# One rotation for queries and keys, moved ahead of the compressions, in a hybrid attention and recurrence kernel

## The chip, the cores and the metric

One core of one Trainium2 chip runs the whole program. The metric is the device time of one execution in microseconds (us), lower is better.

## The reference, cut to what matters

One layer on 1024 tokens of width 1024, float32. A combined projection of the normalised input feeds two groups of eight heads of 64.

```
q, kc, vc, ks, vs, kw, vw, gates, g_nsa, rwkv_in, g_rwkv = split(rms_norm(x) @ w_in)
# group A: three attention branches, 8 query heads, 2 key heads each
k_cmp, v_cmp = compress(kc), compress(vc)        # blocks of 32, stride 16, two-layer MLP
o_cmp = softmax(q @ k_cmp) @ v_cmp               # unrotated q; its weights also pick 8 blocks of 64 keys
o_sel = softmax(rope(q) @ rope(ks) over the picked blocks) @ vs
o_win = softmax(rope(q) @ rope(kw) over the last 512 keys) @ vw
# group B: RWKV-7, a state of 64x64 per head, one step per token (here in chunks of 64)
state = state*w - (state@kk) (kk*a) + v k ;  y = state @ r
out = rms_norm(x + concat(o_nsa*silu(g_nsa), o_rwkv*silu(g_rwkv)) @ w_out)
```

`rope` turns the first 16 of a head's 64 rows: row d becomes `a*cos + w*sin`, where `a` is the row and `w` the row eight further on or back (the sign is in the sine table). The kernel keeps queries and keys in two float32r parts, a high part (`dQH`, `dKH`) and the remainder (`dQL`, `dKL`).

## The kernel before, in words

**Order of the work.** First the normalised input is transposed and a projection of 29 groups of columns begins; each group is 48 matmuls of 512 columns (`p_q`, `p_gn`, `p_gr` and so on), and its weights are fetched in two halves, split in two parts by ScalarE (ACT) and VectorE (DVE). These matmuls are the *filler*: `filler.step(n)` puts n of them at a place in the order of TensorE (PE), `filler.through(name)` all up to a group. The recurrence runs in eight *units* of 128 tokens by half the heads; each unit is a chain of twelve steps (`weave`), each step a few small matmuls (`pc`, `py`) whose results go through DVE and ACT copies (`z`, `x`) before the next step, and after them a half share of the filler, side work, and the other half. Units are counted from 0 in the code (`n`); "the sixth unit" here is n = 6, "the seventh" n = 7, the last.

**Side work.** In unit n < 7 GpSimd (POOL) computes the 31-step triangular recursion of the next unit, two small operations per step on tiles `la`, `lt` and `ltmp` (lines 587 and 589), eight groups of steps with the last three steps at step 5. Its result goes to DRAM (`dT<-lt`) and back (`tt<-dT`), is transposed on DVE (line 633) and enters the matmuls `px` (step 10) and `pt12` (step 11). In units 6 and 7 the two compressions are woven in: each loads two key tiles (`kc2`) and four weight tiles (`w1`), and runs four quarters of 16 matmuls (`pcm`), each behind a pair of additions on DVE and POOL (`xc`). After them, in unit 7, come the rotations: of the keys of both branches (64 rows used), and, started at step 7, of the queries (128 rows). All of these tiles come from one pool of six 4 KB tiles (`c4`), taken in turn.

**What follows.** After unit 7 and its norm a *prologue* loads the queries of the first tile of 128 tokens (`load_queries`: `qt` unrotated, `q1`, `q2`), the keys (`load_keys`) and values, and runs for this tile the compressed branch (`compressed`: matmuls `pcs`, `pct`, `poc`) and the row maxima of both other branches (`row_max`: `pd`, `ps`, reduced on DVE to `bm`), mixed with the filler that is left. Then the attention loop runs over eight tiles in the order `TILES = (1, 5, 4, 3, 6, 2, 7, 0)`; beside each tile it does the compressed branch and the row maxima of the next one, and later the output projection with `w_out`.

**Who sets the order.** In the units the order of PE and POOL is the order in which the program is written; in the prologue and the attention that of PE alone. The other engines, and SP, whose queue issues every DMA, are ordered by a planner that simulates the program; each engine then works strictly in its order. A tile that is placed where an older tile lay waits for the last use of that one.

## Time and profile before

| | |
|---|---|
| median of three runs | 1079.12 us (1078.54 to 1079.7) |
| the profiled execution | 1082.96 us |
| its span, first to last instruction | 1081.2 us |
| PE busy | 936.9 us, 87% of the span |
| DVE, ACT, POOL busy | 579.8, 333.1, 451.6 us |
| mean granted clock of TensorE | 0.934 of full speed |

All rows below are of the profiled execution. "Idle before" is the time in which an engine did nothing ahead of an instruction, with what ended it.

### The profile page before, as it was taken

What the parts mean: (1) busy time and instruction counts of PE and PEld (TensorE: products, weight loads), DVE (VectorE), ACT (ScalarE), POOL (GpSimd) and SP (SyncE); (2) the same over time, 40 slices, a digit from 0 to 9 for tenths busy, and PEclk for the clock granted to TensorE, in tenths of its full rate; (3) what the DMA queues carried; (4) which work ended last, traced back from release to release, by engine and by line L of the source; (5) the groups of instructions that cost most, each with busy time, mean ns of one, the idle gap of its engine ahead of it and who ended that gap; (6) DMA issues with size and microseconds to landing.
All of it is one profiled execution on the core that took longest, in us unless ns stands there. A gap on an engine that the chain in (4) does not pass through costs nothing.

```text
span 1081.2 us, 17166 instructions
## 1 busy us (share of the span) xinstructions
PE 936.9 (87%) x6353; PEld 665.6 (62%) x6353; DVE 579.8 (54%) x1241; ACT 333.1 (31%) x648; POOL 451.6 (42%) x738
## 2 busy tenths in 40 slices
PE   5999999679999899899997619758999999889976
PEld 4888877556766676577775417435555555555555
DVE  7532355344746466464443305447667884776444
ACT  5432323122342434233121101334333344223321
POOL 3100118374555538454513320266545456236521
PEclk9899999689999899899998869879999999899989
DMA  7433344413444355525753395551103132321021
GB/s 248 115 103 111 105 134 135 104 47 102 120 104 122 103 152 139 140 79 138 191 152 112 114 208 114 167 144 59 40 20 98 35 84 50 88 49 56 32 88 39
DMA packets 154381, 114.61 MB, mean 106 GB/s; under 512 B 54961, under 2 KB 132858, under 8 KB 154298
## 3 DMA queue, kind: packets, MB, share of 16 engines
q1 hardware_dynamic: 154298, 113.52, 38.8%
q8 instruction: 50, 0.82, 0.3%
q14 instruction: 33, 0.27, 0.1%
HBM read 76.72 MB, written 33.62 MB: 102 GB/s over the span
## 4 chain that ended last, share of the span: by engine, by line
PE 56%; DMA 13%; POOL 10%; DVE 8%; issue 6%; SPq 5%; ACT 2%; POOLq 0%; DVEq 0%; ACTq 0%
PE pout L113 6%; PE pst L113 6%; SPq L85 5%; PE po L113 5%; PE p_k L113 4%; PE p_r L113 4%; POOL ltmp L587 4%; PE p_v L113 3%; POOL lt L589 3%; PE p_q L113 3%; PE ps L113 2%; PE p_gr L113 2%; PE pd L113 2%; PE pc L113 2%; PE p_gn L113 2%
## 5 line engine op out<-in xcount | busy, mean ns | idle before, releaser
L1038 ACT ACTIVATE prob<-pst 128x512 f32<-128x512 f32 x132 | 74.4, 593 | 115.0 <-PE pst L113 111.4
L587 POOL TENSOR_TENSOR ltmp<-la,lt 128x60 f32<-128x60 f32 (+24 forms) x248 | 84.1, 339 | 51.7 <-DMA la<-dA 27.4
L1051 POOL TENSOR_TENSOR acc<-acc,prob 128x1024 f32<-128x1024 f32 x36 | 85.5, 2375 | 47.6 <-ACT prob L1038 47.5
L589 POOL TENSOR_TENSOR lt<-lt,ltmp 128x60 f32<-128x60 f32 (+24 forms) x248 | 82.5, 333 | 19.0
L113 PE MATMUL pst<-q,k 128*128 128x512 f32 (+1 forms) x264 | 84.3, 437 | 1.3 <-ACT prob L1038 1.2
L990 DVE TENSOR_REDUCE bm<-ps 128x6 f32<-128x384 f32 (+1 forms) x106 | 63.5, 613 | 26.4 <-PE ps L113 25.8
L113 PE MATMUL po<-prob,vt 128*64 128x512 f32 x264 | 74.0, 640 | 0.0
L113 PEld LDWEIGHTS pst<-q,k 128*128 128x128 f32 (+1 forms) x264 | 49.7, 200 | 16.7 <-issue 5.7
L113 PE MATMUL pout<-woh,mh 128*128 128x512 f32 x128 | 57.3, 447 | 0.2 <-DVE xt L1149 0.2
L1051 POOL TENSOR_TENSOR acc<-prob 128x1024 f32<-128x1024 f32 x14 | 33.3, 2378 | 53.1 <-ACT prob L1038 53.1
L113 PE MATMUL ps<-k,q 128*128 128x384 f32 (+3 forms) x136 | 44.9, 382 | 10.5 <-DVE bm L990 9.6
L113 PE MATMUL pout<-wol,mh 128*128 128x512 f32 x128 | 50.8, 397 | 0.0
L113 PE MATMUL pout<-woh,ml 128*128 128x512 f32 x128 | 50.8, 397 | 0.0
L113 PEld LDWEIGHTS ps<-k,q 128*128 128x128 f32 x136 | 24.9, 200 | 36.9 <-DVE bm L990 19.7
L978 DVE TENSOR_REDUCE bm<-pd 128x8 f32<-128x512 f32 x40 | 27.3, 688 | 22.6 <-PE pd L113 22.4
L113 PEld LDWEIGHTS pout<-woh,mh 128*128 128x128 f32 x128 | 24.9, 195 | 20.6 <-issue 17.8
L1130 POOL TENSOR_TENSOR yr<-yr,sg 128x512 f32<-128x512 f32 x8 | 10.8, 1350 | 56.7 <-DMA sg<-dSR 56.7
L683 ACT ACTIVATE x<-pc 64x128 f32<-64x128 f32 x32 | 8.7, 272 | 82.5 <-DVE x L682 80.8
L1073 POOL TENSOR_TENSOR wide<-rr,ones 128x512 f32<-128x512 f32 x16 | 17.5, 1095 | 34.5 <-DVE rr L1069 32.6
L113 PE MATMUL pd<-k,q 128*128 128x128 f32 x160 | 29.6, 309 | 0.0
L113 PE MATMUL pcs<-kcD,qt 128*128 128x128 f32 x64 | 9.6, 295 | 22.9 <-DMA qt<-dQ 22.9
L1065 DVE TENSOR_REDUCE zz<-pz 128x4 f32<-128x512 f32 x32 | 21.8, 685 | 13.4 <-PE pz L1063 13.0
(515 smaller groups left out, 2484.8 us busy)
## 6 DMA issues: line engine op xcount, KB each, us to landing
dM<-mix SPq DMA_DIRECT2D x24, 256.0 KB
q<-dQH SPq DMA_DIRECT2D x22, 256.0 KB
la<-dA SPq DMA_DIRECT2D x32, 128.0 KB
xt<-in_x_dram SPq DMA_DIRECT2D x8, 512.0 KB
out_dram<-xt SPq DMA_DIRECT2D x16, 256.0 KB
x<-in_x_dram SPq DMA_DIRECT2D x7, 512.0 KB
mixr<-dM SPq DMA_DIRECT2D x8, 256.0 KB
mixk<-dM SPq DMA_DIRECT2D x8, 256.0 KB
```

What stands on the lines that cost most here:

```text
L85: return nc.sync.dma_start(plain(o), plain(i))
L113: return T.matmul(o, l, r, start=start, stop=stop)
L587: G.tensor_tensor(tv, la[:, j:j + 1, j + 1:].to_broadcast([128, m, n]), lt[:, :m, j:j + 1].to_broadcast([128, m, n]), op=OP.mult)
L589: G.tensor_tensor(lt[:, :m, j + 1:], lt[:, :m, j + 1:], tv, op=OP.add)
L683: gate["A"] = A.activation(x1[1][HP[1], c:8:4, :], pv[HP[1], :, 64:128], AF.Copy)
L978: V.tensor_reduce(bm[:, g * 4:g * 4 + 4, j:j + 2], p.rearrange("p (r b c) -> p r b c", b=2, c=64), axis=AX.X, op=OP.max)
L990: V.tensor_reduce(bm[:, h0:h0 + n, j:j + 2 * w], p[:, :n * w * 128].rearrange("p (h b c) -> p h b c", h=n, c=64), axis=AX.X, op=OP.max)
L1038: A.activation(pr[:, g * 512:(g + 1) * 512], p, AF.Exp)
L1051: G.tensor_tensor(s, self.acc, pr, op=OP.add)
L1065: V.tensor_reduce(zz[:, g, :], p.rearrange("p (r k) -> p r k", r=4), axis=AX.X, op=OP.add)
L1073: G.tensor_tensor(wide, rr.rearrange("p r g -> p (r g)").unsqueeze(2).to_broadcast([128, 8, 64]), ones64.unsqueeze(1).to_broadcast([128, 8 ...
L1130: G.tensor_tensor(yr, yr, sr, op=OP.mult)
```

## The change

Both rotations become one generator that runs in unit 6, before the compressions, with the two sets (queries in 128 rows, all four key heads in rows 0 to 31 and 64 to 95) sharing one cosine and one sine tile. The rows that are swapped are loaded by halves of all heads at once: 12 loads in place of 31. One product and the sum go to DVE, the high part to ACT; the other product and the remainder stay on POOL, and two memsets fill rows 32 to 63 of the key tiles. The first compression begins at step 7 of unit 6 and the second at step 1 of unit 7. The keys of both branches lie in one DRAM tensor, and `load_keys` loads a branch's two key heads with one DMA per tile. The prologue also loads the second tile's queries and runs its compressed branch, with 30 filler matmuls ahead of the first compressed branch instead of 36; the attention loop leaves that work out for its first tile.

```diff
-    dKH = [dram.tile([128, S], FR, name=f"dKH{b}") for b in range(2)]
...
+    dKHa, dKLa = dram.tile([256, S], FR, name="dKHa"), dram.tile([256, S], FR, name="dKLa")
+    dKFa = dram.tile([256, S], FT, name="dKFa")
+    dKH, dKL, dKF = ([t[b * 128:b * 128 + 128, :] for b in range(2)] for t in (dKHa, dKLa, dKFa))
...
-    def rotate(n, srcs, dhs, dls):
+    def rotate():
...
         ct, sn = c4([128, S], FT, "ropc"), c4([128, S], FT, "rops")
+        sets = []
+        for src, dh, dl in ((dQ, dQH, dQL), (dKFa, dKHa, dKLa)):
+            v = src.rearrange("(h d) t -> h d t", d=64)
+            n = v.shape[0] * 8
+            a, w = c4([128, S], FT, "ropa"), c4([128, S], FT, "ropw")
+            if n < 64:
+                for t in (a, w):
+                    G.memset(t[n:64], 0.0)
+            for hf in range(2):
+                rows = slice(hf * 64, hf * 64 + n)
+                dma(a[rows], v[:, hf * 8:hf * 8 + 8, :])
+                dma(w[rows], v[:, 8 - hf * 8:16 - hf * 8, :])
+            sets.append((slice(0, 64 + n), n, a, w, dh, dl))
         for i, tb in enumerate((ct, sn)):
...
+            for hf in range(2):
+                dma(tb[hf * 64:hf * 64 + 64], rope[i:i + 1, hf * 8:hf * 8 + 8].to_broadcast([8, 8, S]))
+        yield
+        for rows, n, a, w, dh, dl in sets:
+            V.tensor_tensor(a[rows], a[rows], ct[rows], op=OP.mult)
+            G.tensor_tensor(w[rows], w[rows], sn[rows], op=OP.mult)
+            yield
+        for rows, n, a, w, dh, dl in sets:
+            V.tensor_tensor(a[rows], a[rows], w[rows], op=OP.add)
+            h_ = c4([128, S], FR, "roph")
+            A.activation(h_[rows], a[rows], AF.Copy)
+            l_ = c4([128, S], FR, "ropl")
+            G.tensor_tensor(l_[rows], a[rows], h_[rows].bitcast(FT), op=OP.subtract)
+            for d, t in ((dh, h_), (dl, l_)):
+                v = d.rearrange("(h d) t -> h d t", d=64)
+                for hf in range(2):
+                    dma(v[:, hf * 8:hf * 8 + 8, :], t[hf * 64:hf * 64 + n])
+            yield
...
     def load_keys(b):
+        k1 = ka.tile([128, 2, S], FR, name=f"k1{b}")
+        dma(k1[0:64], dKH[b].rearrange("(g d) t -> d g t", d=64))
+        G.tensor_copy(k1[64:128], k1[0:64].bitcast(FT))
+        k2 = ka.tile([104, 2, S], FR, name=f"k2{b}")
+        dma(k2[0:64], dKL[b].rearrange("(g d) t -> d g t", d=64))
+        dma(k2[64:104], dG[b].unsqueeze(1).to_broadcast([40, 2, S]))
...
-                side(call(lambda: comp(0, cmp_w1_k, cmp_w2_k)), 1)
-                for j in (4, 6, 7, 8, 9, 10):
-                    nxt(0)
-                side(call(lambda: comp(1, cmp_w1_v, cmp_w2_v)), 9)
...
+                side(call(lambda: (filler.through("q3"), begin(rotate()))), 1)
+                nxt(0, 4, 5, 6, 7)
+                side(call(lambda: begin(compress(0, cmp_w1_k, cmp_w2_k))), 7)
+                nxt(1, 10, 11)
             if n == 7:
-                for j in (0, 1, 2, 3, 4):
-                    nxt(1)
-                side(call(lambda: rot(4, dKF, dKH, dKL)), 1)
-                for j in (5, 6, 7):
-                    nxt(2)
-                side(call(lambda: (filler.through("q3"), rot(8, [dQ], [dQH], [dQL]))), 7)
-                for j in (9, 10, 11):
-                    nxt(3)
+                nxt(1, 0, 1, 2, 3)
+                side(call(lambda: begin(compress(1, cmp_w1_v, cmp_w2_v))), 1)
+                nxt(2, 4, 5, 6, 7, 8, 9)
...
+        L1 = load_queries(TILES[1], 1)
...
+        com1 = compressed(TILES[1], L1)
+        filler.step(30)
         for gen, n in ((comp, 10), (rm0, 5), (rm0, 5), (comp, 5), (rm0, 5), (rm0, 5), (comp, 5),
-                       (rm1, 5), (rm1, 5), (rm1, 5), (rm1, 5), (rm0, 8), (rm1, 0)):
+                       (rm1, 5), (com1, 5), (rm1, 5), (rm1, 5), (rm1, 5), (rm0, 8), (com1, 5),
+                       (rm1, 5), (com1, 0)):
...
-                    if n < 7:
+                    if 0 < n < 7:
                         side.add(compressed(j, L1), 3, 0.0, 0.9)
```

## Rows read from the trace of the kernel before

**Rows 1.** The page: the span, and PE's busy tenths in 40 slices.

```profile
span 1081.2 us, 17166 instructions
...
PE   5999999679999899899997619758999999889976
```

**Rows 2.** Busy time by stretch: units 6 and 7, then four stages.

```profile
core 0: us, PE busy (x) PEld busy (x) DVE busy (x) ACT busy (x) POOL busy (x), PEclk, DMA share, GB/s
505.86:551.55 45.69, 42.96 (x473) 32.91 (x472) 17.50 (x44) 11.49 (x27) 22.57 (x65) 1.00 0.77 207
551.55:598.54 46.99, 40.74 (x345) 31.95 (x345) 18.71 (x38) 8.38 (x21) 13.61 (x8) 0.93 0.35 101
598.54:624.48 25.94, 15.37 (x62) 11.70 (x60) 10.69 (x20) 2.35 (x4) 12.11 (x11) 0.80 0.40 122
624.48:647.41 22.93, 0.01 (x2) 0.00 (x1) 0.00 (x0) 0.00 (x0) 4.14 (x4) 0.57 0.91 209
647.41:683.08 35.67, 35.62 (x170) 28.07 (x171) 15.77 (x25) 6.87 (x13) 2.02 (x2) 0.94 0.47 100
683.08:726.93 43.85, 22.68 (x77) 11.64 (x75) 23.74 (x43) 15.41 (x22) 22.73 (x13) 0.80 0.62 173
```

**Rows 3.** The chain that ended last: start us, us, what.

```profile
66.29 21.76 PE p_r L113 x96
...
558.38 1.78 PE pcm L113 x16
...
591.63 17.74 DMA dKL<-ropl
...
644.72 9.39 DMA gr2r<-in_w_in_dram
```

**Rows 4.** PE's timeline, units 6 and 7 to the attention: start us, us, instruction.

```profile
527.66 2.05 PE L113 MATMUL pcm<-xc,w 128*128 128x126 f32 x16 [1.73 <-POOL xc L807]
...
545.96 0.69 PE L113 MATMUL px<-t,cr 32*32 32x32 f32 x32
...
584.39 0.69 PE L113 MATMUL pc<-z,tt 64*64 64x64 f32 x8 [6.25 <-DVE z L669]
...
615.62 0.80 PE L113 MATMUL p_gr<-hh,gr1h 128*128 128x512 f32 x1 [10.35 <-ACT gr1h L342]
...
620.64 0.41 PE L113 MATMUL p_gr<-hh,gr1l 128*128 128x512 f32 x1
...
647.41 2.08 PE L113 MATMUL pcs<-kcD,qt 128*128 128x128 f32 x8 [22.92 <-DMA qt<-dQ]
...
689.87 1.09 PE L946 MATMUL pct<-ident,pc 128*128 128x128 f32 x4 [6.16 <-DVE pc L941]
```

**Rows 5.** SP's queue around the second rotation: start us, us issuing, DMA.

```profile
595.69 16.00 SPq L85 DMA_DIRECT2D ropw<-dQ  x14
...
620.71 0.57 SPq L85 DMA_DIRECT2D keep<-in_late_dram  x1
...
636.00 1.58 SPq L85 DMA_DIRECT2D qt<-dQ  x1
```

**Rows 6.** POOL's timeline: lt's end in units 5 and 6, memsets, ropl.

```profile
490.32 0.21 POOL L589 TENSOR_TENSOR lt<-lt,ltmp 128x8 f32<-128x8 f32 x1
...
499.41 0.66 POOL L583 MEMSET tt<- 32x256 f32 x2 [6.66 <-PE pc L113]
...
529.06 0.21 POOL L589 TENSOR_TENSOR lt<-lt,ltmp 128x8 f32<-128x8 f32 x1
...
620.52 2.41 POOL L777 TENSOR_TENSOR ropl<-ropa,roph 128x1024 fp32r<-128x1024 f32 x1
```

**Rows 7.** DVE's timeline, units 5 and 7: start us, us, instruction.

```profile
497.48 0.44 DVE L633 STREAM_TRANSPOSE t<-tt 32x256 f32<-32x256 f32 x1 [0.27 <-DMA tt<-dT]
...
581.31 2.82 DVE L344 TENSOR_TENSOR gr0l<-gr0r,gr0h 128x512 fp32r<-128x512 f32 x1
...
595.01 0.69 DVE L344 TENSOR_TENSOR gr1l<-gr1r,gr1h 128x512 fp32r<-128x512 f32 x1
```

More of the change, by code (lines that the diff above doesn't have):

```diff
@@ L217, in trunk_kernel @@
     dQL = dram.tile([512, S], FR, name="dQL")
-    dKH = [dram.tile([128, S], FR, name=f"dKH{b}") for b in range(2)]
-    dKL = [dram.tile([128, S], FR, name=f"dKL{b}") for b in range(2)]
+    dKHa, dKLa = dram.tile([256, S], FR, name="dKHa"), dram.tile([256, S], FR, name="dKLa")
+    dKFa = dram.tile([256, S], FT, name="dKFa")
+    dKH, dKL, dKF = ([t[b * 128:b * 128 + 128, :] for b in range(2)] for t in (dKHa, dKLa, dKFa))
     dKC = [dram.tile([128, S], FT, name=f"dKC{b}") for b in range(2)]
-    dKF = [dram.tile([128, S], FT, name=f"dKF{b}") for b in range(2)]
     dV = dram.tile([2, S, 128], FT, name="dV")
@@ L857, in load_keys @@
     def load_keys(b):
-        for g in range(2):
-            gs = slice(g * 64, g * 64 + 64)
-            k1 = ka.tile([128, S], FR, name=f"k1{b}{g}")
-            dma(k1[0:64, :], dKH[b][gs, :])
-            G.tensor_copy(k1[64:128, :], k1[0:64, :].bitcast(FT))
-            K1[b, g] = k1
-        for g in range(2):
-            gs = slice(g * 64, g * 64 + 64)
-            k2 = ka.tile([104, S], FR, name=f"k2{b}{g}")
-            dma(k2[0:64, :], dKL[b][gs, :])
-            dma(k2[64:104, :], dG[b])
-            K2[b, g] = k2
+        k1 = ka.tile([128, 2, S], FR, name=f"k1{b}")
[4 more added lines that the diff above has]
+        dma(k2[64:104], dG[b].unsqueeze(1).to_broadcast([40, 2, S]))
+        for g in range(2):
+            K1[b, g], K2[b, g] = k1[:, g, :], k2[:, g, :]
     def load_values(b):
@@ L1326, in trunk_kernel @@
                 nxt_elem = wkv_elementwise(n + 3)
-                side(call(ahead), 6)
+                side(call(ahead), 2)
                 side(nxt_elem, 11)
@@ L1470, in trunk_kernel @@
         for n, i in enumerate(TILES):
-            L1 = None
-            if n < 7:
+            if n == 7:
+                L1 = None
+            elif n:
                 j = TILES[n + 1]
                 L1 = load_queries(j, n + 1)
+            else:
+                j = TILES[1]
             for b in range(2):
@@ L1482, in trunk_kernel @@
                         side.add(row_max(i, 1, L), row_max_pieces(i, 1), 0.0, 0.8)
-                    if n < 7:
+                    if 0 < n < 7:
                         side.add(compressed(j, L1), 3, 0.0, 0.9)
```

43 lines of the change are left out of this document (7 added, 36 removed).

## The prediction, made before the result was known

> **What bounds the kernel now.** I read the page first: a span of 1081.2 us, and in the 40 slices a matrix engine (PE) that is near 9 nearly everywhere, but falls to 6, 1, 9, 7, 5 in slices 22 to 26 [rows 1]. So the kernel is bound by PE, except in one stretch from about 550 to 730 us, and that is the stretch which the change touches. Then I cut that stretch into stages with the busy-time-by-stretch view [rows 2]: the sixth unit of the recurrence keeps PE busy for 42.96 of 45.69 us, the seventh for 40.74 of 46.99. From the seventh unit's end to 624.48 PE works 15.37 of 25.94 us. Then come 22.93 us in which PE does 0.01 us and the transfers run at a share of 0.91 and 209 GB/s. The projection that is left takes 35.67 us, all busy; after it, 22.68 of 43.85 us.
>
> The PE timeline names each hole [rows 4]: 6.25 us (behind the vector engine's copy z), 10.35 us (behind the weights gr1), 22.92 us (behind the load of qt), 6.16 us (behind pc). The queue of SP, which issues every DMA, says why [rows 5]. From 595.69 it spends 16.00 us on 14 small ropw loads of the second rotation, so gr1's second half is late. qt, the first load of the prologue in program order, leaves only at 636.00, after the keys and after the writes of the rotated queries. I read this as space: qt lies where the last rotation tiles lie. That reading can't be seen in a row, and a rival below drops it.
>
> **The change, part by part, in us.** The terms are against the profiled execution: 1082.96 in all, 1.76 outside its span. The median of the plain runs is 1079.12, 3.84 lower; I take that off at the end.
>
> *Sixth unit.* Four quarters of the key compression leave it, 4 x 1.78 [rows 3], with the wait of 1.73 ahead of the first [rows 4]: -8.9. One quarter comes back at step 11: +1.8. What the rotation adds sits on POOL, whose order is fixed by hand and which in this unit runs the 62 small lt operations that end in the next unit's inverse. Two memsets of 32x1024 come in after the fifteenth pair: rows show 0.66 for two of 32x256 [rows 6], so about 2.6. One product of 128x1024 stands before the last three pairs: 2.4, as for ropl [rows 6]. The vector engine's product of 128x1024 holds POOL up too: 1.4, twice the 0.69 of a 128x512 [rows 7]. lt now ends at 529.06 + 0.21 [rows 6]; it would end at 535.7. In the unit before, the second transpose starts 6.95 after lt's end and takes 0.44 [rows 6, 7], so the inverse's px can run at 543.1. PE, freed of 8.9, arrives at 545.96 - 8.9 = 537.1 [rows 4]. That is a new wait of 6.0 (0 at the least, if the small operations hide in POOL's gaps; 7.4 if the second vector product, 1.4, falls before lt's end too). After a hole PE runs at half clock for a while: after the 10.35 us hole, the 10 matmuls from 615.62 to 620.64 took 5.02 [rows 4] where 0.227 each is the running price (21.76 / 96) [rows 3]; of the 2.75 more I take 2.5. Queued behind px on PE is the whole chain of the unit; nobody else waits.
>
> The rotation's POOL part ends at 535.7 + 3 x 2.4 = 542.9. Only then can the compression load into the same six tiles: 1 MB of keys and 0.5 MB of its first weights, at 207 GB/s [rows 2] about 7.6, so 550.5. PE comes to this quarter near 548: a wait of 3 (0 if the planner issues the loads piecewise; 17.7 if a write of the rotation takes what dKL<-ropl took [rows 3]). Sixth unit: -8.9 + 1.8 + 6.0 + 2.5 + 3 = +4.4.
>
> *Seventh unit.* Three quarters come in, 3 x 1.78 = +5.3; the last short steps move with them, no net work. The 6.25 hole goes: z stood behind an operation that took 2.82 instead of 0.69 beside POOL's rotation [rows 4, 7], and behind a load queued after eight small row loads of the keys; there is no rotation in this unit any more. With its half clock, -8.75. Sum -3.4 (+5.3 if the hole stays, from the second compression's nine loads).
>
> *Up to qt.* SP issues 12 loads of 64 rows or fewer instead of 31 small ones, at about the 0.57 of keep's rather than ropw's 1.14 [rows 5], and they come one unit earlier, so gr1 is on time (-10.35) and qt, whose tile the second compression leaves in mid unit, is there before PE asks (-22.92). Two half-clock stretches, -5.0. Six projection matmuls move behind it, -1.4. Sum -39.7. The bound from the other side is the first rival.
>
> *Prologue to the end of the projection.* The six matmuls, +1.4. The second tile's compressed branch: pcs 2.08, pct 1.09 [rows 4] and a third group like pcs, all read at half clock, so about 3 at full: +3. The transfers: keys, values and two tiles' queries are 6 MB; 1 MB can go early, 5 MB at 209 GB/s [rows 2] are 24 us that now run beside PE. In that burst a weight load took 9.39 [rows 3] and has about 7 of cover (20 matmuls at 0.227 and three or four row maxima). Two or three such fetches: +5.5 (0 to 14). Loading keys for both groups at once moves the same bytes with half the issues and one POOL copy of twice the width: nothing, hidden under PE's projection.
>
> *After the projection.* The 6.16 hole and the compressed branch's matmuls (about 4 at half clock) leave: -10.4 at most. But that stage starts with loads into space that only the end of the projection frees, and PE is busy for half of it [rows 2]. So most of what PE gains there it waits again, for POOL and w_out: I take -3 (0 to -10.4).
>
> Sum: +4.4 - 3.4 - 39.7 + 9.9 - 3 = -31.8. 1082.96 - 31.8 - 3.84 = 1047.3, so 1047.
>
> **A rule beside a row.** Two vector operations of the same form, 128x512, took 0.69 and 2.82; the long one ended when POOL's ropl did [rows 7]. The Trainium skill, page "SBUF — State Buffer", section "SBUF: two separate sides", says that a vector operation with two SBUF inputs and a GpSimd operation that reads SBUF exclude each other for a whole instruction. The trace agrees. What it would make of this change is the second rival.
>
> **The rivals.**
> First, *the transfers stay the bound*: the keys still leave before qt. From the first of them, 620.71, to 647.41 are 26.7 us [rows 4, 5]; less 1 MB of query writes at 209 GB/s, 21.7. They cannot start before unit seven's end, and if they start only behind its last norm, near 607, pcs comes at 629 instead of 609. +20, less the 5.5 already charged: -17.3, 1062. For it: the order of SP is a planner's and put qt last before. Against: what it waited behind is gone. 0.14.
>
> Second, *the lock*: POOL's four wide operations, 4 x 2.4, fall where PE works, not inside the wait for px, and each holds the vector engine, with the chain's copies z and x behind it. 9.6 + 2.5 of half clock: 1059. For it: the 6.25 hole. Against: by the times above they run from about 532 to 543, where PE waits for px anyway. 0.10.
>
> Third, *more than I take*: the stage after the projection gives the full 10.4 and the weights are never late: -31.8 - 7.4 - 5.5, 1034 or less. 0.08.
>
> Fourth, the other side, *the rotation's loads come late*. POOL's first product stands in its fixed order ahead of the last lt pairs, near 532; every us it waits for ropa or ropc is a us of px. 2.5 MB queued from about 509 at 207 GB/s [rows 2] are there by 521, ten early. It decides when they come 32 late, near 564: at 570 the time is 1047 + 38, 1085. For it: a 128 KB write of the rotation once took 17.74 [rows 3]; against: even that adds 8. 0.10, of which 0.07 slower and 0.03 within 0.2%, which is about what a measurement of this kernel can tell from no change. The Trainium skill, page "DMA: Bandwidth & Descriptors", section "Why a DMA increments its semaphore by 16 and not by 1", says that a DMA runs on as many engines as divide its slowest dimensions, so a write of two heads would run on two of 16 and one of four heads on four; no row shows single engines, and by it the new key writes would be the shorter.
>
> **How the numbers follow.** The forecast holds 0.58, its own range 1038 to 1057: the sum without px's 6.0 and its half clock on one side, with the weights at 14 on the other. With the first two rivals, 0.82 lie in 1036 to 1069 (the bottom: half way to the third rival; the top: the first rival with the 7 us that px or the compression's loads may add). Faster 0.58 + 0.14 + 0.10 + 0.08 = 0.90, same 0.03, slower 0.07.
>
> **What would show it.** In the profile after: no PE hole over 3 us between unit seven's start and pcs; qt issued before the keys; pcs about 609; in unit six a PE wait for px near 537 with the vector engine's transpose behind dT and tt, and lt's end near 536; the first compression's quarter late by a few us; the end of the projection near 652. Wrong would be: qt still last in SP's queue; a wait for DMA ropa on POOL in the sixth unit; holes in the projection behind gr2 or gr3; or a stage after it that is longer by what came earlier.

## The result, and the profile after

The changed kernel takes 1068.43 us (1067.54 to 1069.83, four runs), the kernel before 1079.41 beside it: a ratio of 0.9897 (95% interval 0.9879 to 0.9915). The forecast was 1047. The direction was right and the top of the range, 1069, just held, but only a third of the gain came. The profiled execution took 1069.83, its span is 1068.0 against 1081.2.

The busy time by stretch, of the kernel after, in the same stages as [rows 2]: unit six, unit seven, the way to pcs, pcs to the end of the projection, the first attention tile, the rest. The columns are stretch, length, then busy time (and instructions) of PE, its weight loads, DVE, ACT, POOL, the granted clock, the DMA share, GB/s.

```profile
502.94:563.30 60.36, 41.26 (x417) 30.60 (x416) 22.22 (x43) 12.42 (x26) 32.03 (x68) 0.86 0.63 173
563.30:607.73 44.43, 44.43 (x401) 35.80 (x401) 16.56 (x43) 9.56 (x24) 6.87 (x13) 1.00 0.45 137
607.73:626.21 18.48, 11.70 (x57) 9.09 (x55) 6.64 (x20) 2.35 (x4) 0.00 (x0) 0.86 0.35 110
626.21:676.70 50.49, 44.03 (x188) 33.29 (x189) 22.74 (x45) 8.90 (x15) 5.80 (x4) 0.85 0.69 141
676.70:735.82 59.12, 40.80 (x166) 22.57 (x165) 43.79 (x65) 23.11 (x35) 38.74 (x20) 0.77 0.56 156
735.82:1068.00 332.18, 302.22 (x1394) 185.73 (x1392) 209.20 (x413) 107.55 (x202) 148.15 (x82) 0.96 0.22 56
```

Set against the forecast's terms (all from profiled executions; the 2.9 us up to unit six lie ahead of the work that was moved, and in the second measurement of the changed kernel that unit began 1.6 us later than in the first):

| stage | before | after | change | forecast |
|---|---|---|---|---|
| up to unit six | 505.86 | 502.94 | -2.9 | 0 |
| unit six | 45.69 | 60.36 | +14.7 | +4.4 |
| unit seven | 46.99 | 44.43 | -2.6 | -3.4 |
| unit seven's end to pcs | 48.87 | 18.48 | -30.4 | -39.7 |
| pcs to the projection's end | 35.67 | 50.49 | +14.8 | +9.9 |
| all behind it | 398.12 | 391.30 | -6.8 | -3 |
| sum | 1081.2 | 1068.0 | -13.2 | -31.8 |

So three stages hold the miss: unit six by 10.3, the way to pcs by 9.3, the prologue by 4.9. PE's timeline of the kernel after names the holes in them; the number in brackets is the idle time ahead of the instruction, with what ended it:

```profile
528.44 0.69 PE L113 MATMUL pc<-x,g 128*64 128x64 f32 x8 [7.09 <-ACT x L690]
...
544.49 0.69 PE L113 MATMUL px<-t,cr 32*32 32x32 f32 x30 [0.22 <-DVE t L633]
...
558.21 3.76 PE L113 MATMUL pcm<-xc,w 128*128 128x126 f32 x16 [9.76 <-DMA w<-in_cmp_w_k_dram]
...
622.86 0.61 PE L113 MATMUL pcs<-cmb,identb 128*128 128x512 bf16 x1 [4.04 <-DVE identb L1379]
...
626.21 2.07 PE L113 MATMUL pcs<-kcD,qt 128*128 128x128 f32 x8 [2.75 <-DMA qt<-dQ]
...
657.31 1.11 PE L113 MATMUL ps<-k,q 128*128 128x128 f32 x4 [4.53 <-DVE bm L981]
```

Behind the first of them stand DVE and POOL. DVE waits 7.96 for the rotation's loads, and x, a copy of the chain, stands behind that product in DVE's order; POOL waits 4.07 at its own product, ahead of the last pairs of lt. The view names the table rops for both. But rops had landed when DVE began, at 526.66, and POOL began at 529.13, at the end of DVE's second product (528.01 + 1.21); in the second measurement (530.86 against 530.83) and in the run with the later quarters (527.64 against 527.61) the two fall together as well. So about 1.6 of the 4.07 are the loads, and the other 2.5 pass while DVE runs its two products:

```profile
526.66 1.23 DVE L776 TENSOR_TENSOR ropa<-ropa,ropc 128x1024 f32<-128x1024 f32 x1 [7.96 <-DMA rops<-in_rope_dram]
527.81 0.28 DVE L689 COPY x<-pc 64x128 f32<-64x128 f32 x1
528.01 1.21 DVE L776 TENSOR_TENSOR ropa<-ropa,ropc 96x1024 f32<-96x1024 f32 x1
...
537.14 3.39 DVE L780 TENSOR_TENSOR ropa<-ropa,ropw 96x1024 f32<-96x1024 f32 x1 [0.42 <-POOL ropw L777]
...
621.78 0.88 DVE L722 SCALAR_TENSOR_TENSOR ny<-ny,cols,nq 128x256 f32<-128x256 f32 x2 [2.64 <-DMA nq<-dS]
622.58 0.22 DVE L1379 CAST identb<-ident 128x128 bf16<-128x128 f32 x1
...
655.96 0.69 DVE L344 TENSOR_TENSOR gr3l<-gr3r,gr3h 128x512 fp32r<-128x512 f32 x1 [11.96 <-ACT gr3h L342]
```

```profile
529.13 2.36 POOL L777 TENSOR_TENSOR ropw<-ropw,rops 128x1024 f32<-128x1024 f32 x1 [4.07 <-DMA rops<-in_rope_dram]
...
534.56 0.21 POOL L589 TENSOR_TENSOR lt<-lt,ltmp 128x8 f32<-128x8 f32 x1
...
537.07 2.38 POOL L784 TENSOR_TENSOR ropl<-ropa,roph 128x1024 fp32r<-128x1024 f32 x1
```

SP's queue shows the order of the transfers. The rotation's first load leaves at 506.57, its last at 514.98 to 517.38. gn2r (the filler's next weights) follows only at 521.63; between 506 and 522 SP stood for 6.2 us in all until older loads of the rotation had ended, before it issued the next. Near the end, dY<-ny stands directly ahead of qt, and the values stand 8 us ahead of the last weights gr3r:

```profile
506.57 0.68 SPq L85 DMA_DIRECT2D ropa<-dQ  x1
...
514.98 2.40 SPq L85 DMA_DIRECT2D rops<-in_rope_dram  x2
...
521.63 2.56 SPq L85 DMA_DIRECT2D gn2r<-in_w_in_dram  x2
...
550.78 0.60 SPq L85 DMA_DIRECT2D dKLa<-ropl  x1
551.81 4.08 SPq L85 DMA_DIRECT2D w<-in_cmp_w_k_dram  x2
...
618.44 0.46 SPq L85 DMA_DIRECT2D nq<-dS  x1
...
622.69 0.37 SPq L85 DMA_DIRECT2D dY<-ny  x1
623.11 0.46 SPq L85 DMA_DIRECT2D qt<-dQ  x1
...
625.66 0.58 SPq L85 DMA_DIRECT2D k<-dKHa  x1
...
639.93 7.99 SPq L85 DMA_DIRECT2D vt<-dV  x2
648.01 2.76 SPq L85 DMA_DIRECT2D gr3r<-in_w_in_dram  x1
```

### The profile page after: what moved, and what is told of

The parts are those of the page before. It is cut to its first block, busy times and chain, and to the rows that moved or that the text cites. A ratio compares the mean times of both kernels' runs of the same rounds, so it can differ in the third digit from the quotient of the medians.

```text
span 1068.0 us, 17143 instructions
## 1 busy us (share of the span) xinstructions
PE 942.7 (88%) x6353; PEld 668.0 (63%) x6353; DVE 585.6 (55%) x1245; ACT 335.5 (31%) x650; POOL 439.9 (41%) x732
## 4 chain that ended last, share of the span: by engine, by line
PE 60%; DMA 11%; POOL 8%; DVE 8%; SPq 5%; issue 5%; ACT 2%; POOLq 0%; DVEq 0%; ACTq 0%
PE pout L113 7%; PE pst L113 6%; PE po L113 5%; SPq L85 5%; PE p_v L113 4%; PE p_q L113 3%; PE p_r L113 3%; PE p_gr L113 3%; PE p_k L113 3%; POOL ltmp L587 3%; POOL lt L589 3%; PE pc L113 3%; PE p_kc L113 3%; PE ps L113 2%; PE p_gn L113 2%
## 5 line engine op out<-in xcount | busy, mean ns | idle before, releaser
L993 DVE TENSOR_REDUCE bm<-ps 128x6 f32<-128x384 f32 (+1 forms) x106 | 63.5, 612 | 27.2 <-PE ps L113 26.7
L113 PE MATMUL po<-prob,vt 128*64 128x512 f32 x264 | 76.7, 661 | 0.0
L1076 POOL TENSOR_TENSOR wide<-rr,ones 128x512 f32<-128x512 f32 x16 | 17.1, 1068 | 35.5 <-DVE rr L1072 33.6
L1152 DVE TENSOR_TENSOR xt<-pout,xt 128x512 f32<-128x512 f32 x16 | 11.1, 691 | 34.1 <-PE pout L113 34.0
L113 PEld LDWEIGHTS pout<-wol,mh 128*128 128x128 f32 x128 | 24.7, 193 | 5.7
```

The source lines that it names most:

```text
L113: return T.matmul(o, l, r, start=start, stop=stop)
L993: V.tensor_reduce(bm[:, h0:h0 + n, j:j + 2 * w], p[:, :n * w * 128].rearrange("p (h b c) -> p h b c", h=n, c=64), axis=AX.X, op=OP.max)
L1076: G.tensor_tensor(wide, rr.rearrange("p r g -> p (r g)").unsqueeze(2).to_broadcast([128, 8, 64]), ones64.unsqueeze(1).to_broadcast([128, 8 ...
L1152: V.tensor_tensor(xt[:, hs], p, xt[:, hs], op=OP.add)
```

## The experiments

The kernel before took 1079 in the first measurement and 1083 to 1086 in the later ones, so versions are compared by their ratio to the runs of it that were taken beside them. The changed kernel, measured once more, gave 0.9868 (0.9843 to 0.9892). Stages below are cut in PE's timeline by the norm's matmul pvar, which is early in the next unit's order: "six" from 505.24 to 564.89 in the kernel after, "seven" from there to 607.73. The stages are of one profiled execution each. In the six that leave unit six as the change has it (both of the change, norm first, gate early, keys by group, no prologue part) it lasts 57.0 to 59.7, and the hole behind x is 4.97 to 7.16: a difference of some 2 us there says nothing by itself.

| version | six | seven | to pcs | projection's end | ratio, interval |
|---|---|---|---|---|---|
| before | 45.0 | 45.4 | 48.9 | 35.5 | 1 |
| changed | 59.7 | 42.8 | 18.5 | 50.5 | 0.9897 (0.9879 to 0.9915) |
| changed, again | 59.3 | 42.9 | 19.2 | 49.4 | 0.9868 (0.9843 to 0.9892) |
| rotation later | 48.8 | 54.8 | 19.1 | 50.2 | 0.9871 (0.9832 to 0.9911) |
| quarters later | 45.1 | 55.3 | 19.2 | 48.9 | 0.9869 (0.9839 to 0.9900) |
| and whole rows | 44.7 | 55.9 | 19.0 | 50.4 | 0.9881 (0.9847 to 0.9915) |
| product on POOL | 63.5 | 42.8 | 18.7 | 50.6 | 0.9903 (0.9878 to 0.9928) |
| tables first | 66.7 | 42.9 | 19.4 | 49.1 | 0.9962 (0.9937 to 0.9987) |
| half the loads | 56.0 | 42.9 | 18.9 | 50.8 | 0.9852 (0.9820 to 0.9884) |
| half, later | 44.7 | 51.2 | 18.4 | 50.1 | 0.9847 (0.9823 to 0.9870) |
| norm first | 58.7 | 42.8 | 18.7 | 49.7 | 0.9882 (0.9838 to 0.9926) |
| gate early | 57.1 | 42.8 | 17.2 | 48.8 | 0.9856 (0.9828 to 0.9883) |
| quarters later, gate early | 43.7 | 55.0 | 17.0 | 48.6 | 0.9818 (0.9790 to 0.9847) |
| one step later still | 44.8 | 55.1 | 17.0 | 49.8 | 0.9805 (0.9782 to 0.9829) |
| that, 48 fillers | 45.7 | 54.3 | 16.9 | 51.0 | 0.9873 (0.9845 to 0.9901) |
| that, two waves | 47.6 | 60.4 | 17.1 | 49.0 | 0.9923 (0.9895 to 0.9952) |
| that, values later | 45.3 | 56.2 | 16.9 | 46.0 | 0.9761 (0.9741 to 0.9781) |
| keys by group | 59.1 | 42.9 | 18.5 | 49.3 | 0.9878 (0.9840 to 0.9917) |
| no prologue part | 57.0 | 42.8 | 18.9 | 47.1 | 0.9940 (0.9916 to 0.9964) |
| before, prologue part | 45.5 | 45.1 | 49.7 | 39.8 | 0.9975 (0.9954 to 0.9996) |

**The sixth unit: rotation later.**

```diff
-                nxt(0, 4, 5, 6, 7)
-                side(call(lambda: begin(compress(0, cmp_w1_k, cmp_w2_k))), 7)
-                nxt(1, 10, 11)
+                nxt(0, 6, 7, 8, 9)
+                side(call(lambda: begin(compress(0, cmp_w1_k, cmp_w2_k))), 9)
```

(and six quarters of the first compression in steps 0 to 5 of unit seven, of the second in 6 to 11)

> The changed kernel with the rotation's work two steps later in the sixth unit (steps 6 to 9 in place of 4 to 7), the first compression begun at step 9, its quarters in steps 0 to 5 of the seventh unit and the second compression's in steps 6 to 11; the same arithmetic. Theory A: the sixth unit lost 7.09 us because the rotation's product stood in DVE's queue ahead of the copy x while the sine table was still landing, and 9.76 us because PE reached the first compression's quarter before its weights were there. Moved back, both waits fall where nothing of the chain is queued behind them: the sixth unit falls from 60.4 to 41 to 44 us, the seventh grows by one or two quarters (1.8 to 3.6), and the time falls by 15 to 21, to about 1050. Theory B: the sixth unit is bound by the volume of its transfers, so the waits move into the seventh unit (compression inputs late there) and the time stays within 5 of the changed kernel, 1064 to 1073.

Measured: 1069.25, theory B. The hole behind x is gone, but PE waits 7.05 for gn2h and 3.86 for gn2l at the same place, and the wait for the compression's weights goes along into unit seven, 8.39.

**Only the quarters later** (the rotation stays at 4 to 7).

> The changed kernel with the rotation where it is (steps 4 to 7 of the sixth unit) and only the compressions' quarters later: the first compression's in steps 0 to 5 of the seventh unit, the second's in steps 6 to 11; the same arithmetic. Theory A: of the sixth unit's loss the 9.76 us are the first quarter reaching PE before its weights, whose tiles are the rotation's own; four to six steps later the weights are there, so that hole goes and the one behind the copy x stays: the sixth unit falls to 46 to 50 us, the seventh grows by 2 to 4, the time falls by 6 to 11, to 1057 to 1063. Theory B: something else that the same transfers delay (a filler's weights, the seventh unit's first copies) takes the place of the wait, as in the run with the rotation itself moved later: 1065 to 1071.

Measured: 1071.79 against 1085.84, a ratio like that of the change itself, as theory B has it. The wait of 9.76 became 3.53 for the weights and 3.03 for gn3h, and units six and seven together lost 2.1 (102.5 to 100.4): less than theory A has, and no measurable gain.

**Whole rows for the tables.**

```diff
-            for hf in range(2):
-                dma(tb[hf * 64:hf * 64 + 64], rope[i:i + 1, hf * 8:hf * 8 + 8].to_broadcast([8, 8, S]))
+            dma(tb, rope[i])
```

> The run with the later quarters, and the cosine and sine tables besides stored with their heads repeated, so that each is one load of 128 whole rows in place of two loads in which eight rows are spread over eight heads; the same bytes reach the tiles, the same arithmetic. Theory A: the burst of the rotation's loads moves at about half of the 16 DMA engines (a share of 0.52 to 0.58) because a load whose slowest dimension is 8 heads runs on 8 engines; whole rows raise the share in that stretch over 0.65, the sine table lands 3 us or more earlier, and the hole of 7.09 behind x shrinks to under 4: 3 to 5 us below the run with the later quarters alone. Theory B: the burst is bound by its bytes or by the issue on SP: the table lands within 1.5 us of where it did and the time stays within 1.5 of that run.

Measured: theory B. The stretch 511 to 517, of the kernel after, then of the run with the later quarters, on which this version is built, and then of this version:

```profile
511.00:517.00 6.00, 6.00 (x65) 4.52 (x65) 3.95 (x15) 0.90 (x3) 5.16 (x13) 1.00 0.52 145
```

```profile
511.00:517.00 6.00, 6.00 (x52) 4.45 (x53) 3.72 (x15) 0.55 (x2) 5.16 (x13) 1.00 0.52 185
```

```profile
511.00:517.00 6.00, 6.00 (x64) 4.52 (x65) 3.67 (x15) 0.82 (x4) 5.16 (x13) 1.00 0.91 173
```

The share rose from 0.52 to 0.91, and the rate did not follow: 145 and 185 GB/s in the two runs without whole rows, 173 with them. DVE's product started at 525.64, against 525.06 in the run with the later quarters alone. The Trainium skill, page "DMA: Bandwidth & Descriptors", section "Why a DMA increments its semaphore by 16 and not by 1", has the number of engines follow from the slowest dimension; the shares agree with it (8 heads against 128 rows), but the landing did not hang on it.

**The product on POOL.**

```diff
-            V.tensor_tensor(a[rows], a[rows], ct[rows], op=OP.mult)
+            G.tensor_tensor(a[rows], a[rows], ct[rows], op=OP.mult)
```

> The changed kernel with the first product of the rotation (rows times cosine) on POOL in place of DVE; the same arithmetic. Theory A: the hole of 7.09 us comes from the place of that product in DVE's queue, ahead of the copy x; on POOL it holds nothing of the chain at once, so the hole ahead of pc at 528 goes, but POOL's fixed order brings lt's end 4 to 5 us later (two products of 2.4) and PE then waits for px: the sixth unit changes by minus 5 to plus 1, the time by the same. Theory B: the copy x is late for another reason (the two-port lock by POOL's product of 4.07): then the hole stays at 5 or more.

Measured: 0.9903, no better. The hole ahead of pc is gone, which theory B rules out and theory A expects. But the wait for px that theory A puts in its place did not come: lt ends at 536.08, 1.3 later, and px waits 0.98. Another wait came, and unit six is 3.8 longer, not 5 shorter to 1 longer. On PE's timeline:

```profile
533.75 0.80 PE L113 MATMUL p_gn<-hh,gn2h 128*128 128x512 f32 x1 [8.85 <-ACT gn2h L342]
```

The weights gn2, queued on SP behind the rotation, are as late as the product was. The wait for the compression's weights is 11.31 here.

**Tables first.** The two tables' loads move ahead of the rows'.

> The changed kernel with the rotation's cosine and sine tables loaded first, ahead of the queries' and keys' rows, in place of last; the same arithmetic. Theory A: the first product needs 2 MB of the 2.5 MB, so it can start about 3 us earlier (by 0.5 MB at 145 GB/s), and the hole of 7.09 ahead of pc shrinks by 2 to 3.5: the time falls by 1 to 4. Theory B: the filler's weights, queued on SP behind the whole burst, are the next to be late at the same place: the wait changes its name and the time stays within 1 of the changed kernel.

Measured: both theories too mild, some 10 us slower than the change (0.9962 against 0.9868). PE waits at both places now, one after the other, and SP and DVE say why: the query rows, issued from 510.47 on, were only there when their product began, at 526.21.

```profile
528.59 0.69 PE L113 MATMUL pc<-x,g 128*64 128x64 f32 x8 [6.03 <-ACT x L690]
...
536.62 0.79 PE L113 MATMUL p_gn<-hh,gn2h 128*128 128x512 f32 x1 [4.28 <-ACT gn2h L342]
```

```profile
510.47 0.58 SPq L85 DMA_DIRECT2D ropa<-dQ  x1
...
526.20 2.54 SPq L85 DMA_DIRECT2D gn2r<-in_w_in_dram  x2
```

```profile
526.21 1.23 DVE L776 TENSOR_TENSOR ropa<-ropa,ropc 128x1024 f32<-128x1024 f32 x1 [8.02 <-DMA ropa<-dQ]
```

Whichever loads come first, the product's last input is there near 526, and the weights wait for SP's turn behind them. From the tenth load on SP waits about two us for older loads ahead of each issue, so that gn2r leaves 4.6 later than in the kernel after.

**Half the loads.**

```diff
-                dma(w[rows], v[:, 8 - hf * 8:16 - hf * 8, :])
...
-        for i, tb in enumerate((ct, sn)):
+        for i, tb in enumerate((ct,)):
...
-            G.tensor_tensor(w[rows], w[rows], sn[rows], op=OP.mult)
+            G.tensor_tensor(w[rows], ct[rows], ct[rows], op=OP.mult)
```

> The changed kernel with half of the rotation's loads left out: the swapped rows and the sine table are not loaded, and POOL's product is cosine times cosine in their place, so the rotation's values are not the reference's; every instruction on DVE, ACT, POOL and PE is there in the same shape. Theory A: the sixth unit's loss is the volume of the rotation's transfers, 2.5 MB at about 145 GB/s from 506.6 to 526.6, in which the product on DVE and the filler's next weights both come late; with 1.25 MB the loads are there by 518, the hole of 7.09 and what stands behind it go, and the sixth unit is 6 to 12 us shorter, the time 1056 to 1062. Theory B: the order on SP and the tiles that the compression takes over from the rotation set the unit's length; then the wait for the compression's weights grows by what the first hole loses, and the time stays above 1064.

Measured: 0.9852, an interval that overlaps those of the change. Unit six is 56.0, 3.7 below the kernel after and 1.0 below the shortest of the six runs that leave it as it is: less than theory A's 6 to 12. The product starts at 519.15 instead of 526.66, so the volume does set the landing, and gn2 is waited for no more: gn2r leaves SP at 510.56 here, 11 us earlier. The compression's weights are still waited for, 7.72, and the wait did not grow as theory B has it. But then ACT's copy x stands behind the rotation's high part roph, which waits for POOL's product at its fixed place behind lt:

```profile
531.84 0.61 PE L113 MATMUL pc<-x,bt 128*64 128x64 f32 x8 [4.51 <-ACT x L683]
```

**Half the loads, and later.**

> The changed kernel with half of the rotation's loads left out (no swapped rows and no sine table, POOL's product is cosine times cosine, so the rotation's values are not the reference's) and the rotation two steps later with the compressions' quarters in the seventh unit, as in the run that moved it later. Theory A: two things of like size hold the sixth unit near 528, one behind the other: the chain's copies behind the rotation's operations on DVE and ACT, and the filler's weights gn2 behind the rotation's loads. Each run so far took away one and met the other (7.09 then 4.51 behind a copy, 8.85 or 7.05 behind gn2); with both taken away no hole over 3 us is left between 510 and 550, and the sixth unit's end is at 544 to 549. Theory B: there is a third wait of that size (the transfers of the next unit's inverse, POOL's order): the unit's end stays at 553 or later.

Measured: theory A in what it says of the holes. One is left in unit six, just over the bound of 3 us that it gave:

```profile
537.67 0.55 PE L113 MATMUL pc<-z,tt 64*64 64x64 f32 x8 [3.08 <-DVE z L669]
```

The cut, pvar, is at 552.15. It stands 1.6 behind the unit's end in the kernel after, and the unit began 2.2 later here, so the end is at 548.4 by the forecast's clock, inside 544 to 549. Against the same schedule with all the loads, units six and seven lost 7.7 (103.6 to 95.9); the ratio did not fall measurably below the change's.

The unit's length is no proof of it, though. It is 44.7 here and 45.1 with the later quarters alone, where holes of 6.16 and 1.04 are still in it. The same matmuls (389) kept PE busy for 39.80 here and 36.55 there, at a granted clock of 0.85 and 0.92: behind the hole of 3.08 PE stood at 0.50, the lower of its two levels (1.2 of 2.4 GHz), from 538 to 551.5. So 3.6 us less of idle time (4.9 against 8.5) came back as 3.3 us of slower work.

**The way to pcs: norm first.** The last norm's three steps in a block of high priority.

> The changed kernel with the three steps of the last unit's norm given precedence in the planner's order; the same arithmetic. Theory A: between the seventh unit's end and pcs 6.8 us are lost (4.04 behind DVE's copy identb and 2.75 behind the load of qt) because both stand behind ny, the product that waits for the recurrence's gate nq, and nq in turn for the norm's matmul pyn, issued 10.0 us after the unit's end. With the norm early, pyn comes within 7 us of the unit's end and both holes shrink to under 3 together: the time falls by 3 to 7, to 1062 to 1065. Theory B: qt, identb and the keys are bound to the space of the units' pool and to the burst of transfers; then pcs moves by less than 1.5 and the time stays within 1.5 of 1068.4.

Measured: 1068.92; the order of the instructions on all engines stayed what it was, so this is one more run of the change and says nothing of either theory.

**The gate early.**

```diff
+        if n == 7:
+            sv = r2("dg", 3, (128, 8, 64)).rearrange("p a b -> p (a b)")
+            dma(sv, dS[n])
...
-        sv = r2("nq", 1)
-        dma(sv, dS[n])
+        if n < 7:
+            sv = r2("nq", 1)
+            dma(sv, dS[n])
```

> The changed kernel with the last norm's load of the gate (nq<-dS) into a tile that is free earlier, so that it no longer follows the matmul pyn; the same arithmetic. Theory A: between the seventh unit and pcs the two holes of 4.04 and 2.75 us both come from ny, which waits 2.64 for that load, with identb behind it on DVE and, on SP, the write of ny and then qt: ny then runs straight behind pyn, qt leaves 2 to 3 us earlier and the two holes fall to 2 to 4.5 together; the time falls by 2 to 4, to 1064 to 1066. Theory B: qt is bound by the space that the units leave, or pcs by the burst: the holes move by under 1 and the time stays within 1.5 of 1068.4.

Measured: pcs comes 17.2 behind unit seven's end instead of 18.5. SP issues qt 12.8 behind it instead of 15.4, so the chain (nq, ny, dY, qt) is as theory A has it:

```profile
618.93 0.42 SPq L85 DMA_DIRECT2D qt<-dQ  x1
```

```profile
618.64 0.39 PE L113 MATMUL pcs<-cmb,identb 128*128 128x512 bf16 x1 [1.44 <-DVE identb L1383]
...
623.35 2.08 PE L113 MATMUL pcs<-kcD,qt 128*128 128x128 f32 x8 [4.32 <-DMA qt<-dQ]
```

But the two holes keep 5.76 of their 6.79, above its bound: qt takes 4.4 to land, where 3.1 did before. The ratio, 0.9856, does not part it from the change; what does is that the way to pcs is 16.9 to 17.2 in all six runs with the gate early and 18.4 to 19.4 in the twelve others of the changed kernel.

**Quarters later and gate early, together.**

> The changed kernel with the later quarters of the compressions and the last norm's gate loaded early, both together; the same arithmetic. Theory A: the two work at different places, so the seventh unit ends near 605 as with the later quarters alone and pcs comes 17 to 18 after it: 1061 to 1065, the fastest so far. Theory B: what the one gains at pcs the transfers behind it take back: no faster than either alone, 1065 to 1069.

Measured: 1063.03, theory A: 0.5% below the change in its second measurement (the intervals overlap by 0.0004), 0.8% below the first (they lie apart).

**One step later still.**

> The fastest run so far (later quarters, gate loaded early) with the first compression's quarters one step later still (steps 1, 1, 2, 3, 4, 5 of the seventh unit, the second's begun at step 4 and in steps 6 to 11); the same arithmetic. Theory A: the first quarter still met a wait of 3.76 for its weights, which land about 556.6; four us later nothing is waited for and the time falls by 2 to 4 against that run. Theory B: the filler's weights gn3, late in the same burst, take the place of that wait (2.11 there already): within 1.5 of that run.

Measured: 1063.74, theory B. The wait for the compression's weights stays 3.28 and that for gn3h 1.61.

**48 fillers ahead of pcs.**

> The same with 48 in place of 30 filler matmuls ahead of the first compressed branch; the same arithmetic. Theory A: pcs waits 4.05 us for qt and 1.44 for identb; 18 matmuls of 0.227 are 4.1 us that PE can run there, and as the filler still has matmuls left at the end of the prologue, they are not missed: pcs starts where it did, and the projection ends 3 to 5 earlier. Theory B: the fillers are missed behind pcs, where they cover the maxima and the weights gr3 (holes of 2.70 and 4.26 there): what is gained ahead of pcs is lost after it, within 1.5 of the run without.

Measured: 1070.37, theory B and worse. pcs starts where it did, 16.9 behind the unit's end, with a hole of 1.37 ahead of it in place of 1.44 and 4.14. But what the fillers covered behind it opens (1.82 and 3.86 before), and the stage up to the projection's end is 1.2 longer. That is a small part of the 0.7% between the ratios; another 2.3 lie behind the projection, and the rest is spread over the stages ahead or not explained.

```profile
632.49 0.66 PE L113 MATMUL pd<-k,q 128*128 128x128 f32 x4 [4.08 <-POOL k L871]
...
654.21 0.58 PE L113 MATMUL pd<-maskb,identb 128*128 128x512 bf16 x1 [9.03 <-DVE bm L997]
```

**The rotation's loads in two waves.**

> The version with the quarters one step later still and the gate loaded early, with the rotation's loads besides in two waves: tables and query rows (2 MB) at step 1 of the sixth unit, the key rows (0.5 MB) at step 4, the products at steps 5 and 7, the sums at 8 and 9, the first compression from step 9 and its quarters from step 2 of the seventh unit; the same arithmetic. Theory A: loads in flight share one rate, so with 0.5 MB less beside them the first product's inputs and the filler's weights gn2 come 3 us earlier: the hole near 528 (6.00) shrinks to under 3.5 and no hole behind gn2 opens: 1 to 4 less than that version's 1063.7. Theory B: the key rows and the later sums now delay the compression's weights and gn3 by as much: within 1.5 of it, or slower.

Measured: 1074.94, theory B. The hole behind x went; 10.73 behind gn2h and 12.38 behind gn3h took its place:

```profile
534.48 0.80 PE L113 MATMUL p_gn<-hh,gn2h 128*128 128x512 f32 x1 [10.73 <-ACT gn2h L342]
...
569.17 0.80 PE L113 MATMUL p_gn<-hh,gn3h 128*128 128x512 f32 x1 [12.38 <-ACT gn3h L342]
```

**The prologue: values later.**

```diff
-        load_values(0)
-        load_values(1)
...
+        load_values(0)
+        load_values(1)
...
-        dma(t, dV[b].rearrange("(n p) c -> p n c", p=128))
+        behind(dma(t, dV[b].rearrange("(n p) c -> p n c", p=128)), filler.groups[-1].last)
```

(moved behind the prologue's loop; `last` is DVE's split of gr3's first half)

> The version with the quarters one step later still and the gate loaded early (1063.7), with the two loads of the values (1 MB, vt) besides held back until DVE has split the first half of the last weights gr3, so that gr3 leaves SP ahead of them; the same arithmetic. Theory A: behind pcs the projection waits 3.86 us for the maximum bm, which stands on DVE behind gr3's second part, and gr3 was queued on SP behind the values (8 us on SP, 7.2 to land): without them it leaves 6 to 8 us earlier, the hole goes, and the projection's end comes 3 to 5 us earlier, the time is 1058 to 1061. Theory B: gr3 then meets the second tile's queries in flight, or the values are late for the attention's first product: within 1.5 of 1063.7, or slower.

Measured: 1059.38 against 1085.14, 0.9761: theory A. gr3r leaves 6.4 us earlier than in the version without the edit (644.29), DVE's split waits 7.46 instead of 11.30, no hole over 2 us is left between pcs and the projection's end, and that stretch is 45.96 where the version without the edit has 49.77. The stage behind it is 3.0 shorter too (386.6 against 389.6); why is open. Against that version's ratio, 0.9805, the intervals only just lie apart (0.9781 and 0.9782).

```profile
637.88 4.60 SPq L85 DMA_DIRECT2D gr3r<-in_w_in_dram  x1
```

```profile
649.84 0.69 DVE L344 TENSOR_TENSOR gr3l<-gr3r,gr3h 128x512 fp32r<-128x512 f32 x1 [7.46 <-ACT gr3h L342]
```

**The other two parts alone.** Keys loaded by group, in the changed kernel:

> The changed kernel with the keys loaded for each group alone again (12 loads and four copies on POOL in place of six and two); the same arithmetic. Theory A (as forecast): the same bytes, hidden: the time stays within 2 of the changed kernel. Theory B: in the burst behind pcs each issue on SP counts: six more at about 0.57 put the second tile's queries, the values and the weights gr3 3.4 later, and the projection's end with them: 1070 to 1073.

Measured: 0.9878, theory A: nothing. Without the prologue part:

> The changed kernel without its prologue part: the second tile's queries are loaded and its compressed branch runs beside the first tile of the attention loop, and 36 filler matmuls stand ahead of the first compressed branch, as in the kernel before. Theory A (as forecast): the part moves about 3 us of matmuls and 1 MB of loads ahead and takes a hole of 6 and half-clock matmuls out of the first tile; the prologue falls by 3 to 9 and the first tile grows by 8 to 10, so without it the time is 1067 to 1074, a gain of the part between 0 and 5. Theory B: what the prologue part costs (the weights gr3 late behind six loads of queries) is more than it brings; then the time without it is 1060 to 1066.

Measured: 0.9940, so the part brings 0.4 to 0.7% (against 0.9897 and 0.9868), 5 to 8 us and more than theory A's 5 at its top. By stages: pcs to the projection's end is 47.1 without it, 49.4 to 50.5 with it; all behind is 401.2 without it, 391.3 to 393.1 with it. On the kernel before:

> The kernel before with the prologue part alone: the second tile's queries loaded in the prologue, its compressed branch there, 30 filler matmuls ahead of the first compressed branch. Theory A: qt still leaves last, so that six filler matmuls (1.4 us) fewer cover its wait, the second tile's loads queue behind the keys, and the first tile of the attention loses its hole of 6: between 1070 and 1079, within 5 of the kernel before. Theory B: the prologue, which has no transfers to spare, loses 5 to 10 behind gr2 and gr3: 1080 to 1086.

Measured: 1080.00 against 1082.81, 0.9975. As a ratio that is theory A (1077 where the kernel before takes 1079.4), as a plain time it lies at theory B's edge. From unit seven's end to the projection's end it loses 5.2 (84.3 to 89.5), and behind that it gains 5.9 (398.3 to 392.4). The loss is not theory B's: between pcs and the projection's end PE has no hole, it is busy for all of 39.83 us at a granted clock of 0.93. The added work alone is 4.2.

**The change again.**

> The changed kernel itself, as it is, once more beside the kernel before and beside the versions with edits: it gives the change's ratio on this chip. Theory A: the ratio of the first measurement, 0.9897, holds within its interval (0.988 to 0.9915). Theory B: the kernel before is slower here (1083 in place of 1079), mainly where transfers set its end, and the change with fewer waits for transfers is worth more: 0.982 to 0.987.

Measured: 0.9868, inside theory B's numbers; the two intervals overlap between 0.9879 and 0.9892, and why the kernel before is slower there is open.

## Why the prediction was wrong

*Sixth unit, +4.4 against +14.7.* Two steps failed, and the rows divide the 10.3 between them. Up to px: lt ends at 534.77, which is 31.8 into the unit (forecast 29.8), because POOL's product waited 4.07: about 1.6 for the loads, which I had put at nothing, and 2.5 while DVE ran both its products, of which I had charged one at 1.4. The two memsets took 1.9 of the 2.6 that I gave them. From there to px it took 9.7 instead of 7.4. Together px came 4.3 late. The wait did not show as one for px, as PE had already stood 7.09 behind x. Behind px: the first quarter waited 9.76, not 3, of which 6.0 remain once the rest is set off. I had 1.5 MB land in 7.6 us behind the rotation's end. Counted from the unit's start, that end came at 41.1 (forecast 37.0), and the last of the weights landed 14.0 behind it, at 558.1. They lie in the tiles that the rotation writes out, and between the loads of two of them SP waited 3.2 for such a write (dKHa<-roph; the row at 551.81).

The root of the first part is a term that I put into the fourth rival and dismissed: 2.5 MB "there by 521, ten early". They left from 506.57 on and were there at 526.6: 20 us, where I had taken 12 at the 207 GB/s of [rows 2], so about 125 GB/s. I gave it a price only through POOL's fixed order. The price came by two other ways: DVE's and ACT's order, which the planner set, with the chain's copies behind the rotation's operations; and SP's order, with the filler's weights behind the twelve loads. Either alone costs some 7 to 11 us at the same place, so they do not simply add: the run on POOL and the later rotation took away the first and met the second, the halved loads the second and met a part of the first. With the tables first both were there, one behind the other (6.03 and 4.28). Only half the loads and the later rotation together left a single hole, of 3.08.

*Seventh unit, -3.4 against -2.6.* Right: no hole, PE busy all of it, at full clock.

*Up to qt, -39.7 against -30.4.* gr1's wait went and qt leaves SP ahead of the keys, as forecast. The step that failed is "there before PE asks". qt's place in SP's order is right behind dY<-ny (as I read it, the last use of the units' pool), and ny waits for its gate; so 4.04 and 2.75 are left, and moving the gate's load moved qt's issue. That accounts for 6.6 (6.8, less 0.2 of small gaps that were there before). The other 2.7 are work: PE's busy time there fell by 3.7 (15.38 to 11.70), where I took 6.4 for the half clock and the six moved matmuls.

*Prologue, +9.9 against +14.8.* The holes are 6.5 (forecast 5.5). PE's busy time grew by 8.4, not 4.4. My 4.4 for the work was right: in the kernel before with the prologue part alone, with no hole, it is 4.2. The other 4.2 are the clock: it is 0.85 in this stretch, 0.94 before, it stands near 0.50 from 634.5 to 638 and from 655 to 662, at the two holes, and I had charged no half clock there. The weights gr3 were the right suspect, and their place behind the values was the cause of the hole at 657: with the values held back that hole is gone and the stretch is 46.0, near the 45.6 forecast.

*Behind the projection, -3 against -6.8.* Mis-sized. The prologue part gives 8 to 10 there in the changed kernel (401.2 against 393.1 and 391.3) and 5.9 in the kernel before, nearer to the bound of 10.4 than to the 3 to which I had cut it for fear of POOL and w_out.

*The rivals.* The first named the right brake in part (loads that start only behind the last norm), but with keys ahead of qt, which did not happen (its 620.71 is the row of keep; the first key load left at 621.32). The second, the lock, is in the trace without a hole of its own on PE: the sum of 96x1024 took 3.39 at 537.14 beside POOL's ropl (537.07 + 2.38), and 1.17 at 544.03 in the run with the rotation later; the other way round it is the likely cause of the 2.5 us for which POOL's product stood beside DVE's. In the kernel before, the ropl beside which the 2.82 of [rows 7] fell is this one:

```profile
581.19 2.40 POOL L777 TENSOR_TENSOR ropl<-ropa,roph 64x1024 fp32r<-64x1024 f32 x1
```

The fourth came true in mechanism, about 8 us late in place of the 32 from which I let it decide. Of the signs of being wrong that I had listed two came: POOL's wait for a load of the rotation, and a hole in the projection behind gr3. That 1069, the top of the range, held is luck: the bound stood for the first rival, which did not happen.

What stays open: why the burst moves at 145 to 185 GB/s (511 to 517 us) where [rows 2] show 207 and the kernel after itself 230 to 260 between 545 and 565; a DMA share of 0.91 in place of 0.52 did not raise it. Why SP waits for older loads that share no tile with the next is open too.

## What to carry to other kernels

When an edit moves a bundle of loads, ask of every engine what stands behind the first operation that uses them, the transfer queue included: here DVE, ACT, POOL and SP each held something of the critical chain, and a fix of one only showed the next. Space is worth the same question: what must be written out of a tile before the next load enters it (the compression's weights, 3.2 us of SP's time), and, as I read it for qt without having shown it, what must end before a load can start. A hole costs more than its length: what PE does behind it can run at half clock, 13.5 us of it behind a hole of 3.08. The gains that held came from loading the gate early together with the later quarters, and from taking bulk that is not urgent (the values) out of the way of weights that are.

## What the runs showed of the hardware

In the burst a load of 256 KB took long to land: the query rows, issued at 510.47 to 511.73 in the run with the tables first, were there at 526.2, some 15 us later, where qt took 3.1 from issue to pcs. With half the bytes in the burst the first product began 7.5 us earlier; with the same bytes and the tables first it began 0.5 earlier (526.21), and with whole rows 0.6 later than in the run that it was built on (525.64 against 525.06). And the DMA share was no measure of the rate: 0.52 stood for 145 and for 185 GB/s, 0.91 for 173.

The time that TensorE spent at its lower clock did not follow the length of the hole ahead of it: behind 3.08 us it was granted 0.50 from 538 to 551.5 (half the loads, later), behind 6.16 us it was back at full speed by 531, 4.2 us after the hole's end (quarters later).
